# LayerNorm of a residual sum on one core: adds moved to GpSimd, ScalarE and VectorE put into hardware loops

## The chip, the cores and the metric

The kernel runs on one core of one Trainium2 chip. The metric is the time on the device, in microseconds (us), of the slowest (here the only) core. A run is one execution; medians are over several runs of one kernel.

## The reference

```python
# x, residual: 16 x 1024 x 512 float32; gamma, beta: 512
z = x + residual
mean = np.mean(z, axis=-1, keepdims=True)
var = np.var(z, axis=-1, keepdims=True)
return (gamma * (z - mean) / np.sqrt(var + eps) + beta).astype(np.float32)
```

There are 16384 rows of 512 values. Each of the 128 partitions handles 128 of them, so a "row" below means one row in every partition, a tile of 128 x 512. Both inputs are read and the result is written: 100.66 MB pass between the core's SBUF and memory, whatever the kernel does in between. (SBUF is the core's on-chip buffer; PSUM is the one into which TensorE's matmuls write.)

## The kernel before

One buffer holds 64 rows of x, is overwritten by the sum and at last by the result, and is stored from there. Another holds 32 rows of the residual. All large transfers are issued from one queue (SP), loads 40 rows ahead of the stores.

```python
X_CHUNKS = [8] * 15 + [4, 4]      # rows of one load; R_CHUNKS is the same
OUT_CHUNKS = [16] * 7 + [8, 4, 4] # rows of one store
GROUP = 4; Z_ROWS = 64; R_ROWS = 32; STORE_LAG = 40; ADD_PERIOD = 8
```

Seven rows of eight are added by TensorE: two matmuls with an identity matrix sum x and residual in PSUM. ScalarE copies the sum back to SBUF and takes the row's total on the way. The eighth row is added on VectorE.

```python
def add(g):
    ...
        nc.tensor.matmul(ps, ident, zrow(j), start=True, stop=False)
        nc.tensor.matmul(ps, ident, rrow(j), start=False, stop=True)

def copy_then_sqrt(g):
    ...
        nc.scalar.activation(out=zrow(j), in_=PS.pop(j), func=ACT.Identity,
                             accum_out=SM[g][:, j - j0 : j - j0 + 1])
```

VectorE makes the negated mean of four rows. ScalarE squares the centred rows and sums them. VectorE then makes two passes over every row, (z - mean) * gamma and z * rstd + beta, with gamma and beta in SBUF.

```python
def affine1(g):
    ...
        nc.vector.scalar_tensor_tensor(out=zrow(j0 + k), in0=zrow(j0 + k),
            scalar=NM[g][:, k : k + 1], in1=gamma_t, op0=ALU.add, op1=ALU.mult)

def affine2(g):
    ...
        nc.vector.scalar_tensor_tensor(out=zrow(j0 + k), in0=zrow(j0 + k),
            scalar=rstd[:, k : k + 1], in1=beta_t, op0=ALU.mult, op1=ALU.add)
```

Everything is written out: Python loops emit each instruction of all 128 rows.

## Time and profile before

| | before |
|---|---|
| time, median of 3 runs | 242.99 us (242.69 to 243.09) |
| bytes moved by the large transfers | 100.67 MB |
| share of the 16 DMA engines' span in those transfers | 98.1% |
| last load landed (the one before it: 205.9 us) | 210.8 us |
| last VectorE pass ended | 231.2 us |
| end of the profiled execution | 241.0 us |

First come lines of the profile's page of the kernel before. The line "PE 203.2 ..." gives busy time and share of the span by engine, with the number of instructions. DMA cuts the span into 40 slices and gives the busy share of the DMA engines in tenths. The q lines are DMA queues: packets, MB, share of the 16 engines' span. The line with "DVE 53%" is the chain of waits that ended last. Group lines give busy time, mean ns of one, and the engine's idle time before them with what ended it.

```profile
span 241.0 us, 1990 instructions
...
PE 203.2 (84%) x452; PEld 87.6 (36%) x452; DVE 192.7 (80%) x356; ACT 169.8 (70%) x514; POOL 0.7 (0%) x6
...
DMA  7999999999999999999999999999999999999993
...
q1 hardware_dynamic: 6336, 100.67, 98.1%
q8 instruction: 3, 0.05, 0.1%
q14 instruction: 7, 0.06, 0.1%
...
DVE 53%; DMA 19%; PE 17%; issue 3%; ACT 3%; SPq 1%; DVEq 0%
...
L209 DVE SCALAR_TENSOR_TENSOR zbuf<-zbuf,nm,gamma_t 128x512 f32<-128x512 f32 x128 | 89.5, 749 | 12.8 <-ACT junk L185 12.8
...
L224 DVE SCALAR_TENSOR_TENSOR zbuf<-zbuf,rstd,beta_t 128x512 f32<-128x512 f32 x128 | 87.7, 747 | 1.1
...
```

TensorE is busy for 84% of the span, but it does not set the time. The DMA row is at 9 from the second slice to the last but one, and queue q1 alone fills 98.1%. Queues q8 and q14, of the kind "instruction" on the page, move 0.11 MB at 0.1% of the 16 engines' span each. They are called instruction fetches below; e2 and e3 fit that (loops written out took q14 from 2 packets to 6, and a stream of TensorE instructions brought q8 back).

Next is the windows view of the kernel before. A window's columns are its length, busy time of each engine with the number of instructions, TensorE clock, DMA share (1.00 is all 16 engines busy), GB/s.

```profile
...
core 0: us, PE busy (x) PEld busy (x) DVE busy (x) ACT busy (x) POOL busy (x), PEclk, DMA share, GB/s
12.00:226.00 214.00, 197.12 (x446) 86.08 (x446) 185.99 (x344) 168.33 (x513) 0.00 (x0) 0.98 1.01 430
226.00:229.00 3.00, 0.00 (x0) 0.00 (x0) 2.96 (x6) 0.15 (x1) 0.00 (x0) 0.50 0.87 371
236.00:237.00 1.00, 0.00 (x0) 0.00 (x0) 0.00 (x0) 0.00 (x0) 0.00 (x0) 0.50 0.62 262
237.00:238.00 1.00, 0.00 (x0) 0.00 (x0) 0.00 (x0) 0.00 (x0) 0.00 (x0) 0.50 0.37 156
238.00:239.00 1.00, 0.00 (x0) 0.00 (x0) 0.00 (x0) 0.00 (x0) 0.00 (x0) 0.50 0.18 74
...
```

Over 214 us the DMA engines are full (a share of 1.01, 430 GB/s). The last view of this kernel is the SP queue's own waits (total, times, longest).

```profile
...
SPq L81 <- DMA out_dram<-zbuf: 92.6, 4, 27.0
SPq L84 <- DVE zbuf L140: 55.8, 5, 14.9
SPq L87 <- DVE zbuf L224: 44.3, 4, 20.7
...
```

SP waits longest for stores to land, because a load may only overwrite rows that have been stored. It also waits for VectorE (L84 and L87), so this view alone does not settle what binds; with the DMA share of 1.01 it fits a full queue. The chain of waits, which names VectorE first, then names work that hides behind transfers.

### The profile page before, as it was taken

The numbers are of one execution on the slowest core, as the hardware profiler recorded it, in microseconds if no ns is written. First come the engines' busy times: TensorE is split into PE (matmuls) and PEld (weight loads), VectorE is DVE, ScalarE is ACT, GpSimd is POOL, SyncE is SP. The second block draws the span as 40 slices with busy tenths as digits, with TensorE's granted clock in tenths as the row PEclk, the third lists the DMA queues.
The fourth block names the chain that finished last, engine by engine and source line by source line (L and its number), as shares of the span: only waits on it lengthen the run. The fifth ranks groups of instructions, "written<-read, shape, count | busy, mean of one in ns | idle before, by whom it ended". The sixth has DMA issues, their size and how long they took to land.

```text
span 241.0 us, 1990 instructions
## 1 busy us (share of the span) xinstructions
PE 203.2 (84%) x452; PEld 87.6 (36%) x452; DVE 192.7 (80%) x356; ACT 169.8 (70%) x514; POOL 0.7 (0%) x6
## 2 busy tenths in 40 slices
PE   3689999999999999999999996899949999890000
PEld 0134444444444444444444442344414444340000
DVE  1101279999999999999999999739997799989930
ACT  0213699797979797979797979269783888786500
POOL 1000000000000000000000000000000000000000
PEclk9999999999999999999999999799999999997555
DMA  7999999999999999999999999999999999999993
GB/s 262 435 435 435 430 422 419 423 432 431 435 443 432 400 428 432 430 430 430 431 432 443 426 419 427 427 468 405 419 432 430 450 401 419 443 435 435 427 413 160
DMA packets 6350, 100.78 MB, mean 418 GB/s; under 512 B 706, under 2 KB 706, under 8 KB 708
## 3 DMA queue, kind: packets, MB, share of 16 engines
q1 hardware_dynamic: 6336, 100.67, 98.1%
q8 instruction: 3, 0.05, 0.1%
q14 instruction: 7, 0.06, 0.1%
q10 hardware_dynamic: 4, 0.00, 0.0%
HBM read 67.11 MB, written 33.55 MB: 418 GB/s over the span
## 4 chain that ended last, share of the span: by engine, by line
DVE 53%; DMA 19%; PE 17%; issue 3%; ACT 3%; SPq 1%; DVEq 0%
DVE zbuf L209 26%; DVE zbuf L224 23%; DMA rbuf<-in_residual_dram 19%; PE ps L133 9%; PE ps L132 8%; DVE zbuf L140 3%; ACT junk L185 1%; DVE rstd L222 1%; ACT zbuf L156 1%; DVE nm L171 1%; ACT L197 1%; SPq L81 0%; DVEq L312 0%; SPq L87 0%; ACT std L197 0%
## 5 line engine op out<-in xcount | busy, mean ns | idle before, releaser
L133 PE MATMUL ps<-rbuf,ident 128*128 128x512 f32 x224 | 117.5, 607 | 9.4 <-DVE zbuf L209 6.4
L132 PE MATMUL ps<-zbuf,ident 128*128 128x512 f32 x224 | 117.6, 607 | 0.0
L209 DVE SCALAR_TENSOR_TENSOR zbuf<-zbuf,nm,gamma_t 128x512 f32<-128x512 f32 x128 | 89.5, 749 | 12.8 <-ACT junk L185 12.8
L156 ACT ACTIVATE zbuf<-ps 128x512 f32<-128x512 f32 x112 | 66.0, 589 | 46.6 <-PE ps L133 46.5
L185 ACT ACTIVATE junk<-zbuf,nm 128x512 f32<-128x512 f32 x128 | 90.4, 711 | 1.6 <-DVE nm L171 1.6
L224 DVE SCALAR_TENSOR_TENSOR zbuf<-zbuf,rstd,beta_t 128x512 f32<-128x512 f32 x128 | 87.7, 747 | 1.1
L133 PEld LDWEIGHTS ps<-rbuf,ident 128*128 128x128 f32 x224 | 43.0, 194 | 66.4 <-issue 53.0
L132 PEld LDWEIGHTS ps<-zbuf,ident 128*128 128x128 f32 x224 | 43.6, 195 | 56.3 <-issue 43.3
L185 ACT ACTIVATION_READ_ACCUMULATOR junk<-zbuf,nm 128x1 f32 x128 | 24.3, 190 | 0.0
L156 ACT ACTIVATION_READ_ACCUMULATOR zbuf<-ps 128x1 f32 x112 | 21.8, 195 | 0.0
L171 DVE TENSOR_SCALAR nm<-sm 128x4 f32<-128x4 f32 x32 | 5.2, 163 | 13.3 <-ACT zbuf L156 13.3
L140 DVE SCALAR_TENSOR_TENSOR zbuf<-zbuf,rbuf 128x512 f32<-128x512 f32 x16 | 11.0, 685 | 0.0
L197 ACT ACTIVATE std<-ssq,eps_t 128x4 f32<-128x4 f32 x32 | 9.3, 290 | 0.1
L222 DVE RECIPROCAL rstd<-std 128x4 f32<-128x4 f32 x32 | 5.6, 175 | 3.2 <-ACT std L197 3.2
L115 PE MATMUL ps<-gb_row,ones 1*128 1x512 f32 x4 | 4.1, 1129 | 4.8 <-DMA gb_row<-in_gamma_dram 2.7
L156 ACT ACT_TABLE_LOAD x1 | 1.3, 1283 | 8.1 <-DMA zbuf<-in_x_dram 8.1
L116 DVE COPY gamma_t<-ps 128x512 f32<-128x512 f32 x1 | 0.7, 692 | 3.8 <-PE ps L115 3.8
L116 DVE COPY beta_t<-ps 128x512 f32<-128x512 f32 x1 | 0.7, 692 | 3.5 <-PE ps L115 3.5
L115 PEld LDWEIGHTS ps<-gb_row,ones 1*128 1x128 f32 x4 | 1.0, 306 | 6.3 <-DMA gb_row<-in_beta_dram 3.6
L140 DVE DVE_READ_ACCUMULATOR zbuf<-zbuf,rbuf 128x1 f32 x16 | 1.3, 82 | 0.0
L197 ACT ACT_TABLE_LOAD x1 | 1.3, 1283 | 0.0
L104 DVE MEMSET ones<- 1x128 f32 x1 | 0.2, 165 | 0.8 <-PEq L298 0.8
(7 smaller groups left out, 1.0 us busy)
## 6 DMA issues: line engine op xcount, KB each, us to landing
zbuf<-in_x_dram SPq DMA_DIRECT2D x15, 2048.0 KB, 25.3
rbuf<-in_residual_dram SPq DMA_DIRECT2D x15, 2048.0 KB, 20.8
out_dram<-zbuf SPq DMA_DIRECT2D x7, 4096.0 KB, 28.7
zbuf<-in_x_dram SPq DMA_DIRECT2D x2, 1024.0 KB, 33.1
rbuf<-in_residual_dram SPq DMA_DIRECT2D x2, 1024.0 KB, 33.1
out_dram<-zbuf SPq DMA_DIRECT2D x1, 2048.0 KB, 15.5
out_dram<-zbuf SPq DMA_DIRECT2D x2, 1024.0 KB, 10.2
gb_row<-in_gamma_dram ACTq DMA_DIRECT2D x1, 2.0 KB
```

Of the source, the lines that this page charges most:

```text
L115: nc.tensor.matmul(ps, ones, gb_row[:, k, :], start=True, stop=True)
L116: nc.vector.tensor_copy(dest, ps)
L132: nc.tensor.matmul(ps, ident, zrow(j), start=True, stop=False)
L133: nc.tensor.matmul(ps, ident, rrow(j), start=False, stop=True)
L140: nc.vector.scalar_tensor_tensor(out=zrow(j), in0=zrow(j), scalar=0.0, in1=rrow(j), op0=ALU.add, op1=ALU.add, accum_out=SM[g][:, j - j0 : ...
L156: nc.scalar.activation(out=zrow(j), in_=PS.pop(j), func=ACT.Identity, accum_out=SM[g][:, j - j0 : j - j0 + 1],)
L171: nc.vector.tensor_scalar(out=nm[:, :n], in0=SM.pop(g)[:, :n], scalar1=-inv_d, scalar2=None, op0=ALU.mult,)
L185: nc.scalar.activation(out=junk, in_=zrow(j0 + k), func=ACT.Square, bias=NM[g][:, k : k + 1], accum_out=ssq[:, k : k + 1],)
L197: nc.scalar.activation(out=std[:, :n], in_=SSQ.pop(g)[:, :n], func=ACT.Sqrt, bias=eps_t[:, 0:1], scale=inv_d,)
L209: nc.vector.scalar_tensor_tensor(out=zrow(j0 + k), in0=zrow(j0 + k), scalar=NM[g][:, k : k + 1], in1=gamma_t, op0=ALU.add, op1=ALU.mult,)
L222: nc.vector.reciprocal(out=rstd[:, :n], in_=STD.pop(g)[:, :n])
L224: nc.vector.scalar_tensor_tensor(out=zrow(j0 + k), in0=zrow(j0 + k), scalar=rstd[:, k : k + 1], in1=beta_t, op0=ALU.mult, op1=ALU.add,)
```

## The change

The transfers, their order and the buffers are the same. The work on rows is divided anew. GpSimd adds a whole loaded chunk in place. ScalarE reads each row twice from SBUF, first for the negated mean and then for the squares, and writes the unneeded full-size results to PSUM. VectorE has gamma and beta in PSUM, where matmuls with ones put them. TensorE does nothing after that. ScalarE and VectorE run hardware loops of 16 turns of 8 rows, each with its head placed by `head_slot`. Semaphores are counted by hand. (The diff is cut, and some lines are joined.)

```diff
-    for j in range(j0, j0 + n):              # add, rows not on VectorE
-        nc.tensor.matmul(ps, ident, zrow(j), start=True, stop=False)
-        nc.tensor.matmul(ps, ident, rrow(j), start=False, stop=True)
...
+    while lo < total:
+        nc.gpsimd.wait_ge(sx[have_x], 16)
+        nc.gpsimd.wait_ge(sr[have_r], 16)
+        nc.gpsimd.tensor_tensor(
+            out=z, in0=z, in1=part(rbuf, R_ROWS, lo, n), op=ALU.add
+        ).then_inc(s_add, n)
...
+    with act.bass.Fori(
+        0, turns, engines=OrderedEngineSet([act.engine]), head_slot={act.engine: 128}
+    ) as t:
+        ...
+        act.wait_ge(s_add, r0 + TURN)
+        for k in range(2 * TURN):
+            ...
+            if k < TURN:
+                i = act.activation(out=junk[k % JUNK][:, :], in_=row_at(zoff, row),
+                    func=ACT.Identity, scale=-inv_d, accum_out=nm[:, bass.ds(r0 + row, 1)])
+            else:
+                i = act.activation(out=junk[k % JUNK][:, :], in_=row_at(zoff, row),
+                    func=ACT.Square, bias=nm[:, bass.ds(r0 + row, 1)],
+                    accum_out=ssq[:, bass.ds(r0 + row, 1)])
+            i.then_inc(s_act, 1).wait_op(s_act, due, "sem-ge")
+        ...                                   # Sqrt of 8 rows
...
+    with dve.bass.Fori(
+        0, turns, engines=OrderedEngineSet([dve.engine]), head_slot={dve.engine: 128}
+    ) as t:
+        ...                                   # first pass, reciprocal, second pass
-                in1=gamma_t,
+                in1=gamma_p[:, :],
...
-                in1=beta_t,
+                in1=beta_p[:, :],
```

## The prediction

> **What bounds the kernel now.** The transfers. The page's list of DMA queues puts 98.1% of all 16 engines' span on one queue, 100.67 MB in 241.0 us. The windows view shows the DMA share at about 1.00, 426 to 437 GB/s, in nearly every stretch from 12 to 226 us; only the start, 226 to 229 us (0.87) and the last five microseconds (0.62 falling to 0.00) are below. 100.67 MB at 430 GB/s is 234 us. The chain of waits names VectorE (53%), but its 192.7 us of work hide behind the full DMA queue: the store queue's longest waits are for stores to land (92.6 us). The last loads land at 205.9 us, VectorE's last row is done at 231.2, and the DMA stays full until 236.
>
> **What the change removes, adds and moves.** 448 matmuls, 112 ScalarE copies out of PSUM and 16 VectorE adds go. GpSimd adds whole chunks of 8 rows. ScalarE makes the negated mean in a scaled Identity pass, then Square, both from SBUF to PSUM. VectorE keeps two passes per row, gamma and beta now in PSUM. The 44 large transfers and their order are unchanged.
>
> Cost of 8 rows (estimates):
> - GpSimd: [...] No such add is in the trace. [...]
> - ScalarE: Square starts every 0.705 us in the timeline, Identity from PSUM every 0.57, from SBUF perhaps 0.62. 8 x 1.32 + 0.2 for the root = 10.8 us.
> - VectorE: four passes take 2.65 us on the chain, 0.66 each. [...] plus 0.6 for reciprocal, waits and loop turn: about 12 us.
> - DMA: 6.29 MB at 430 GB/s: 14.6 us.
>
> So every engine stays under the DMA's pace. [...]
>
> **On the critical path.** Nearly nothing in the middle: the first output comes later, but some 15 us of queued loads stand before the first store. At the tail, from the last landing at about 206 us: [...] Identity 5, Square 6, plus the backlog of the turn before; I expect VectorE to end at about 233 us, so the last store starts some 2 us later, partly hidden by queued stores. Saved: 0.3% of DMA time of instruction fetch, and the 0.4 us dip at 226.
>
> **Predicted: 242.8 us, 240.5 to 248 in 8 of 10; faster by over 2% 0.03, within 2% 0.84, slower 0.13.**
>
> **What will show it.** Right: DMA about 98% and 1.00 in the middle windows; [...] ScalarE near 170 us, VectorE 170 to 195, PE near 0; VectorE ending at 231 to 235. Wrong: DMA share below 0.95 before 220 us; 1 us idle or more at each loop turn.
>
> **What would make it wrong.** VectorE above about 13 us per turn [...]: then VectorE ends after 240 us and the time follows. Faster than 240 only if the final drain shortens.

Cut from the recorded text, where marked, is what no trace of this case showed when it was written: the cost of GpSimd's add, per chunk and at the tail, a surcharge for VectorE's PSUM sources, the reason for gamma and beta in PSUM, a sentence on loop turns, and suspected causes of failure. The sums still contain these terms, so what stands does not add up to them. The turn of VectorE came to about 12 us: 16 passes at the 0.66 us of the trace make 10.6, 0.6 is the estimate for the reciprocal, waits and the loop's turn, with no source given, and the surcharge came on top. The upper end of 195 us busy contains it too. VectorE's end came to about 233 us, with the add, and with a backlog for which no figure was given. That GpSimd stays under the transfers' pace was shown only by the changed kernel (8.86 us per chunk).

## The result, and the profile after

Four runs of the changed kernel had a median of 242.07 us (241.97 to 242.40), and four of the kernel before, in the same rounds, 243.04 us (242.69 to 243.32). The ratio is 0.9968, with a 95% interval from 0.9953 to 0.9984. Ratios here are those that the timing program gave, worked out from the fast runs of the same rounds; they are not quite the ratios of the medians (here 0.9960) or of the plain means (0.9963) of these runs. The change is faster by 0.3%: the same within 2%, but clear of noise.

The page of the changed kernel, the same lines as before:

```profile
span 240.3 us, 1855 instructions
...
PE 4.1 (2%) x4; PEld 1.0 (0%) x4; DVE 178.7 (74%) x274; ACT 176.6 (73%) x529; POOL 142.1 (59%) x21
...
DMA  7999999999999999999999999999999999999994
...
q1 hardware_dynamic: 6336, 100.67, 98.3%
q14 instruction: 2, 0.02, 0.0%
...
DMA 56%; ACT 14%; issue 13%; POOL 6%; DVE 3%; SPq 2%; ACTq 2%; DVEq 0%; POOLq 0%
...
L158 POOL TENSOR_TENSOR zbuf<-zbuf,rbuf 128x4096 f32<-128x4096 f32 (+1 forms) x17 | 141.9, 8348 | 72.2 <-DMA rbuf<-in_residual_dram 72.2
L221 DVE SCALAR_TENSOR_TENSOR zbuf<-zbuf,nm,gamma_p 128x512 f32 x128 | 91.0, 748 | 51.5 <-ACT junk L193 50.0
...
L234 DVE SCALAR_TENSOR_TENSOR zbuf<-zbuf,rstd,beta_p 128x512 f32 x128 | 85.7, 743 | 0.6
...
```

The two VectorE groups take 0.75 us per pass, as before. GpSimd's line mixes 15 adds of 4096 columns with two of 2048; by form they took 8858 and 4524 ns. No compute engine is busy for more than 74% of the span. The DMA row and the 98.3% of q1 are as before. Instruction fetch is down to one line with 0.02 MB. The chain of waits now names transfers.

The windows view of the changed kernel (columns as before):

```profile
...
12.00:226.00 214.00, 0.00 (x0) 0.00 (x0) 172.76 (x263) 175.31 (x528) 141.92 (x17) 1.00 1.01 430
226.00:229.00 3.00, 0.00 (x0) 0.00 (x0) 2.96 (x6) 0.00 (x0) 0.00 (x0) 1.00 0.89 382
236.00:237.00 1.00, 0.00 (x0) 0.00 (x0) 0.00 (x0) 0.00 (x0) 0.00 (x0) 1.00 0.80 336
237.00:238.00 1.00, 0.00 (x0) 0.00 (x0) 0.00 (x0) 0.00 (x0) 0.00 (x0) 1.00 0.14 57
238.00:239.00 1.00, 0.00 (x0) 0.00 (x0) 0.00 (x0) 0.00 (x0) 0.00 (x0) 1.00 0.04 16
...
```

The middle is unchanged. The dip at 226 to 229 us is still there. The difference is after 236 us: the engines stop nearer to each other. Before, shares of 0.37 and 0.18 were left in the two microseconds after 237; now they are 0.14 and 0.04.

The SP queue's own waits of the changed kernel:

```profile
...
SPq L131 <- DMA out_dram<-zbuf: 111.2, 4, 29.7
SPq L145 <- DVE zbuf L234: 65.2, 7, 29.0
SPq L137 <- POOL zbuf L158: 35.9, 4, 17.0
...
```

SP waits a little longer in total for stores to land (111.2 us against 92.6 us). Waits for compute have grown too, but the queue behind them was never empty in the windows above.

**Where the 0.8 us came from.** Each large transfer raises its semaphore in 16 steps, and the trace has the time of every step. I take the steps to be one for each of the 16 DMA engines: the same distances come back in transfer after transfer (the two largest are 2.6 and 3.0 us in each of the last four loads of e2). I call the distance of the last of the 16 from their median the lag. It tells how far the most delayed DMA engines are behind the rest. The final store of 1 MB ends the program, so its last step counts and not its median. I worked the following table out of the traces (all in us from the first instruction; "fetches" are instruction-fetch packets of 8 KB or more that began between 12 and 237 us).

```
kernel             median step   last step   lag    span     fetches
before                237.06       239.88    2.82   240.96   10, of these 3 of 16 KB
changed               237.32       239.05    1.73   240.33    1
```

The bulk of the final store landed 0.26 us later in the changed kernel (its first load was issued at 0.94 us, before at 0.74). Its last step landed 0.83 us earlier, because the lag is 1.09 us shorter. That is the whole gain, and a little more. (Lags are read from one profiled run of each kernel. The changed kernel gave 1.73 us here and 1.51 us in e9, so differences of a few tenths mean nothing.) Six of the 16 steps were more than 1.3 us behind the median before, and two are now.

I took two theories to the chip. **Theory A**: instruction fetches take time on the same DMA engines (in the kernel before, packets of 8 KB took 0.31 to 0.33 us between 12 and 237 us, those of 16 KB 1.00 to 1.10 us); in a kernel that keeps the engines full, a delayed one never catches up, and the program ends with the most delayed one. **Theory B**: the gain comes from the new division of the work, with TensorE silent and another order of work at the end.

### The profile page after: what moved, and what is told of

Read it like the earlier page. It is cut to its first block, busy times and chain, and to the rows that moved or that the text cites. A ratio compares the mean times of both kernels' runs of the same rounds, so it can differ in the third digit from the quotient of the medians.

```text
span 240.3 us, 1855 instructions
## 1 busy us (share of the span) xinstructions
PE 4.1 (2%) x4; PEld 1.0 (0%) x4; DVE 178.7 (74%) x274; ACT 176.6 (73%) x529; POOL 142.1 (59%) x21
## 3 DMA queue, kind: packets, MB, share of 16 engines
q1 hardware_dynamic: 6336, 100.67, 98.3%
## 4 chain that ended last, share of the span: by engine, by line
DMA 56%; ACT 14%; issue 13%; POOL 6%; DVE 3%; SPq 2%; ACTq 2%; DVEq 0%; POOLq 0%
DMA out_dram<-zbuf 36%; DMA rbuf<-in_residual_dram 20%; ACT junk L193 9%; POOL zbuf L158 6%; ACT junk L185 5%; DVE zbuf L234 3%; SPq L131 1%; ACTq L183 1%; ACTq L185 1%; SPq L137 1%; ACT std L202 0%; SPq L145 0%; DVE rstd L230 0%; DVEq L234 0%; ACTq L171 0%
## 5 line engine op out<-in xcount | busy, mean ns | idle before, releaser
L158 POOL TENSOR_TENSOR zbuf<-zbuf,rbuf 128x4096 f32<-128x4096 f32 (+1 forms) x17 | 141.9, 8348 | 72.2 <-DMA rbuf<-in_residual_dram 72.2
L221 DVE SCALAR_TENSOR_TENSOR zbuf<-zbuf,nm,gamma_p 128x512 f32 x128 | 91.0, 748 | 51.5 <-ACT junk L193 50.0
L185 ACT ACTIVATE junk<-zbuf 128x512 f32 x128 | 74.5, 582 | 46.0 <-POOL zbuf L158 43.0
L193 ACT ACTIVATE junk<-zbuf,nm 128x512 f32 x128 | 86.2, 674 | 0.0
L234 DVE SCALAR_TENSOR_TENSOR zbuf<-zbuf,rstd,beta_p 128x512 f32 x128 | 85.7, 743 | 0.6
L193 ACT ACTIVATION_READ_ACCUMULATOR junk<-zbuf,nm x128 | 24.2, 189 | 0.0
L185 ACT ACTIVATION_READ_ACCUMULATOR junk<-zbuf x128 | 23.9, 187 | 0.0
L202 ACT ACTIVATE std<-ssq,eps_t x16 | 4.8, 301 | 1.6
L230 DVE RECIPROCAL rstd<-std x16 | 3.1, 196 | 0.0
L110 PE MATMUL beta_p<-gb_row,ones 1*128 1x512 f32 x2 | 2.1, 1136 | 2.4 <-DMA gb_row<-in_beta_dram 2.4
```

The lines of the kernel that those rows point to most:

```text
L110: nc.tensor.matmul(dest[:, :], ones[:, :], gb_row[:, k * D : (k + 1) * D], start=True, stop=True).then_inc(s_pe, 1)
L158: nc.gpsimd.tensor_tensor(out=z, in0=z, in1=part(rbuf, R_ROWS, lo, n), op=ALU.add).then_inc(s_add, n)
L185: i = act.activation(out=junk[k % JUNK][:, :], in_=row_at(zoff, row), func=ACT.Identity, scale=-inv_d, accum_out=nm[:, bass.ds(r0 + row, 1)],)
L193: i = act.activation(out=junk[k % JUNK][:, :], in_=row_at(zoff, row), func=ACT.Square, bias=nm[:, bass.ds(r0 + row, 1)], accum_out=ssq[:, ...
L202: act.activation(out=std[:, bass.ds(r0, TURN)], in_=ssq[:, bass.ds(r0, TURN)], func=ACT.Sqrt, bias=eps_t[:, 0:1], scale=inv_d,).then_inc(s ...
L221: dve.scalar_tensor_tensor(out=row_at(zoff, k), in0=row_at(zoff, k), scalar=nm[:, bass.ds(r0 + k, 1)], in1=gamma_p[:, :], op0=ALU.add, op1 ...
```

## The experiments

Eleven kernels were run, all with repeated timing against the kernel before on the same chip. Each edit is against the changed kernel.

### e1: the transfers alone

```diff
-            wait_rows(s_add, "add", rlo + rn - R_ROWS)   # and: wait_rows(s_out, "out", olo + on)
+            # wait for the landing of the loads that used these rows
-    (all GpSimd, ScalarE and VectorE work on rows)
```

> The changed kernel without its compute (wrong result on purpose): the same 44 large transfers in the same order, each waiting only for the landings it depends on. If both kernels are bound by the transfers (theory A and B alike): 241.2 to 242.2 us, at most 1 us under the changed kernel's 242.07, DMA share 98% or more. If compute holds back the changed kernel somewhere: 238 us or less. Theory A (instruction fetches delay single DMA engines, and the last store ends with the most delayed engine) expects a lag of the last of the 16 landings of the final store behind their median of 1.8 us or less (1.73 in the changed kernel, 2.82 in the one before).

Measured: 241.25 us (241.21 to 241.34), ratio 0.9933; lag 0.42 us. Its output is wrong, which doesn't matter for the time. Lines of its page:

```profile
span 239.2 us, 126 instructions
...
q1 hardware_dynamic: 6336, 100.67, 98.7%
...
q14 instruction: 1, 0.00, 0.0%
...
```

The floor of these transfers in this order is 241.25 us. The changed kernel stands 0.8 us above it and the kernel before 1.7 us. With this order of transfers and these waits between them, that is all that a change to the compute alone could gain. The bulk of the final store landed at 237.32 us, exactly as in the changed kernel; all of the difference between the two last steps is lag.

### e2: both loops written out

```diff
-    with act.bass.Fori(0, turns, ..., head_slot={act.engine: 128}) as t:
+    for t in range(turns):
-    with dve.bass.Fori(0, turns, ..., head_slot={dve.engine: 128}) as t:
+    for t in range(turns):
```

> The changed kernel with both hardware loops written out; same division of the work, same semaphores. Theory A (the 0.8 us come from fewer instruction fetches, which ride on the DMA engines): about six more fetches of 8 KB, each 0.3 to 0.6 us of delay to the engine that carries it; lag of the final store 2.0 to 2.6 us, time 242.3 to 242.9. Theory B (the 0.8 us come from the other division of the work: TensorE idle, no SBUF or PSUM traffic of matmuls, another tail): no loop is needed, time 241.9 to 242.2, lag as in the changed kernel.

Measured: 243.12 us (243.06 to 243.36), ratio 1.001; lag 2.96 us, six fetches. Correct. Lines of its page:

```profile
span 241.4 us, 1004 instructions
...
q1 hardware_dynamic: 6336, 100.67, 97.9%
q14 instruction: 6, 0.05, 0.0%
...
```

This is the division of the work of the changed kernel, and all of its gain is gone. Theory B falls. The size was larger than I expected of theory A (243.12 against at most 242.9): 0.05 MB of fetches cost 1 us. The steps can be watched. This table, worked out of the trace, gives for each fetch the two largest distances from the median in the transfer that landed before it or as it began, and in a transfer that landed soon after it (us):

```
fetch of 8 KB at   before        after
 37.5              0.16  0.19    0.16  0.58
 59.6              0.15  0.57    0.55  0.94
 81.6              0.55  1.11    1.15  1.36
118.6              1.58  1.62    1.58  2.31
147.7              1.57  2.31    2.31  2.56
176.4              2.29  2.56    2.56  2.98
```

Each of the six fetches is followed by a step, and in the loads no distance is made up for later. Two things do not fit a simple sum. The steps, 0.4 to 1.0 us for each fetch over the two engines, are longer than the 0.31 us that a fetch packet itself took in the trace. And there are rises with no recorded fetch beside them: one from 0.94 to 1.11 at about 72 us, and one from 1.16 and 1.36 to 1.56 and 1.63 at about 100 us. Whether the trace holds every fetch is not known.

### e3: an idle instruction stream on TensorE

```diff
+    for c in range(len(loads_x)):
+        nc.tensor.wait_ge(sx[c], 16)
+        for k in range(13):
+            m = nc.tensor.matmul(pe_junk[:, :1], ones[:, :], gb_row[:, :1], start=True, stop=True)
```

> The changed kernel plus 221 one-column matmuls on the otherwise idle TensorE, 13 after each landed chunk of x, written to a spare PSUM bank: about the number of TensorE instructions of the kernel before (some 880), nothing waits for them. Theory A: three or four more fetches of 16 KB, which cost the engine that carries one up to 1.6 us: lag 2.2 to 3.3 us, time 242.4 to 243.2. Theory B: 241.9 to 242.2, because these matmuls move almost no data.

Measured: 242.64 us (242.39 to 242.91), ratio 0.9991; lag 2.17 us. Correct. The 1.6 us of the expectation fits the kernel before: from the load that landed at 47.0 us to that at 51.9 us (medians) the lag there went from 0.14 to 1.65 us, with a fetch of 8 KB at 45.3 us and one of 16 KB at 47.3 us. Three packets of 16 KB on q8 came back, a queue that the changed kernel does not use. Adding instructions that do nothing useful, move almost no data and delay no transfer took away more than half of the gain by the ratios; the intervals still touch (0.9979 to 1.0003 here, 0.9953 to 0.9984 for the changed kernel). This run also keeps TensorE busy for 101 us, so by itself it does not tell fetches from an active TensorE; e2 and e11, with TensorE idle, do. The first 16 KB fetch, at 42.5 us, was followed by a step from under 0.1 to 1.53 us on one engine. The latest engine rose to 2.1 us between 67 and 72 us with no recorded fetch beside it, and the two later fetches left its distance as it was.

### e4: both

The edits of e2 and e3 together.

> Loops written out and the idle TensorE stream, both: the number of fetched instructions of the kernel before with the division of the work of the changed one. Theory A: the whole gain is gone, 242.7 to 243.4 us, lag 2.5 to 3.3 us. Theory B: 241.9 to 242.2.

Measured: 242.98 us (242.96 to 243.29), ratio 1.0008 to the kernel before, whose runs of the same rounds had a median of 242.98 too; lag 2.44 us, nine fetches. Correct. The instruction traffic of the kernel before, on the changed division of work, gives the time before. With nine fetches it is not slower than e2 with six. That fits that the most delayed engine counts and not the sum of the fetches; the trace does not name the engine that carried a fetch.

### e5: a small add

```diff
-        z = part(zbuf, Z_ROWS, lo, n)
+        z = part(zbuf, Z_ROWS, lo, n)[:, :16]
-            out=z, in0=z, in1=part(rbuf, R_ROWS, lo, n), op=ALU.add
+            out=z, in0=z, in1=part(rbuf, R_ROWS, lo, n)[:, :16], op=ALU.add
```

> The changed kernel, but each GpSimd add covers 16 columns of its chunk and not 4096 (wrong result on purpose): the chain stays, the GpSimd work of 8.9 us per chunk goes. If the lag that is left in the changed kernel (1.73 us, against 0.42 without any compute) comes from GpSimd's traffic in SBUF: lag 0.4 to 0.9 us, time 241.2 to 241.7. If it comes from the instruction fetches at the loops' start and from something that GpSimd has no part in: lag 1.4 to 1.9 us, time 241.8 to 242.3. That the compute ends some 4.5 us earlier is worth nothing in either, if the transfers bind.

Measured: 242.18 us (242.05 to 242.46), ratio 0.9953; lag 2.13 us. Its output is wrong, which doesn't matter for the time. The lag in the profiled run, the slowest of the five (242.46 us), was larger than either branch expected: a miss. GpSimd's traffic is not its source, since the lag is there without it. Taking 8.9 us of latency out of each chunk's chain bought nothing beyond the noise.

### e6: gamma and beta in SBUF

```diff
+    dve.tensor_copy(gamma_t[:, :], gamma_p[:, :]).then_inc(s_copy, 1)
+    dve.tensor_copy(beta_t[:, :], beta_p[:, :]).then_inc(s_copy, 1)
+    dve.wait_ge(s_copy, 2)
-                in1=gamma_p[:, :],        # and beta_p
+                in1=gamma_t[:, :],        # and beta_t
```

> The changed kernel with gamma and beta copied from PSUM to SBUF, so VectorE's passes read two tensors from SBUF beside GpSimd. [...] VectorE and GpSimd block each other, a VectorE pass waits up to 8.9 us for a chunk's add, a turn of VectorE goes from 11.3 to 16 us or more, and the time to 255 us or more. [...] the GpSimd add 10 to 14 us, VectorE passes up to 1 us, time within 242 to 250. If there is no contention: 242.0 to 242.3, and PSUM was not needed for that.

The first branch has each engine wait for the other's whole work, the second has them take turns.

Measured: 331.47 us (331.34 to 331.65), ratio 1.3625. Correct. Groups of instructions by form, as on the page:

```profile
...
L240 DVE SCALAR_TENSOR_TENSOR zbuf<-zbuf,rstd,beta_t 128x512 f32 x128 | 179.1, 1471 | 0.6
L158 POOL TENSOR_TENSOR zbuf<-zbuf,rbuf 128x4096 f32<-128x4096 f32 x15 | 149.5, 9976 | 96.5 <-DMA rbuf<-in_residual_dram 96.5
L227 DVE SCALAR_TENSOR_TENSOR zbuf<-zbuf,nm,gamma_t 128x512 f32 x128 | 115.7, 974 | 18.3 <-ACT junk L193 18.3
...
```

And its timeline (start, us, instruction, count):

```profile
...
118.26 5.38 DVE L227 SCALAR_TENSOR_TENSOR zbuf<-zbuf,nm,gamma_t 128x512 f32 x8
...
118.78 13.53 POOL L158 TENSOR_TENSOR zbuf<-zbuf,rbuf 128x4096 f32<-128x4096 f32 x1 [36.81 <-DMA rbuf<-in_residual_dram]
...
123.80 9.06 DVE L240 SCALAR_TENSOR_TENSOR zbuf<-zbuf,rstd,beta_t 128x512 f32 x1
```

One VectorE pass, which takes 0.75 us undisturbed, took 9.06 us, as long as a GpSimd add. One add, begun while VectorE was in a row of passes, took 13.53 us and not 8.86. The add waited for the whole row of passes, which ended at 123.6 us, and the next pass then waited for the whole add: it ended at 132.9 us, 0.55 us after it. So they do not take turns pass by pass. Over the run, 16 passes took more than 1 us (4.6 to 9.3), and the four adds that began in a row of passes took 11.1 to 13.5 us. The page of this run shows what that did to the transfers:

```profile
...
DMA  7999999960029999999008999999404990822966
...
q1 hardware_dynamic: 6336, 100.67, 73.0%
...
```

The DMA share fell from 98% to 73%. So gamma and beta in PSUM are what lets GpSimd add without loss beside these passes: with them there, adds took 8.86 us and passes 0.743 and 0.748 us on average. Expected was 255 us or more; how much more was not worked out, so the 331 us was not predicted.

### e7: a slower ScalarE

```diff
+EXTRA = 4
-        for k in range(2 * TURN):
+        for k in range(EXTRA + 2 * TURN):      # the first EXTRA passes write to a spare column
```

> The changed kernel with 4 more sum passes (0.61 us each) per turn on ScalarE, results thrown away: a turn of 13.8 us, still below the transfers' 14.6 us. If only the mean pace counted: time as in the changed kernel, 242 to 243. As predicted (above about 13 us per turn the time follows, because ScalarE starts at 22 us and has 16 turns to do): ScalarE ends near 243 us, VectorE near 249 us, time 253 to 258.

Measured: 255.79 us (255.71 to 256.32), ratio 1.0519. Correct. VectorE ended at 248.9 us, where 249 had been expected. ScalarE's turn of 13.8 us was shorter than the 14.6 us that the transfers take for 8 rows (6.29 MB at the measured 430 GB/s), and the kernel still became bound by compute. ScalarE begins only after the first chunk has landed and been added, at 22.9 us, and 16 turns of 13.8 us from there end after the transfers.

### e8: loop heads not placed

```diff
-        0, turns, engines=OrderedEngineSet([act.engine]), head_slot={act.engine: 128}
+        0, turns, engines=OrderedEngineSet([act.engine])        # the same for VectorE
```

> The changed kernel without the placing of the loop heads. Theory A: [...]more fetches than the 8 of the changed kernel, by up to 30, lag 2.5 us or more and time 242.8 or more, with ScalarE or VectorE idle of 1 us or more at the turns. [...]no more fetches, 241.7 to 242.3. Theory B (division of the work): 241.9 to 242.3 in either case, as long as the turns stay below 13 us.

The first branch of theory A has more fetches without the placing, the second (241.7 to 242.3 us) has no more.

Measured: 242.40 us (242.22 to 242.50), ratio 0.9962; lag 1.61 us, one fetch. Correct. The time lies 0.1 us above the branch without more fetches, but the kernel before was slower in these rounds as well (243.24 us), and the ratio equals that of the changed kernel. Here the placing was worth nothing; no run shows a case in which it pays.

### e9, e10, e11: what is left

e9 is the changed kernel once more. e10 runs the loops of the changed kernel beside the transfers of e1 on buffers of their own:

```diff
+    za, zv, zw: buffers of 1, 8 and 8 rows; R_ROWS = 16 to make room
-                    in_=row_at(zoff, row),
+                    in_=za[:, :],
-                out=row_at(zoff, k), in0=row_at(zoff, k),
+                out=zv[:, k * D : (k + 1) * D], in0=za[:, :],      # second pass: zw
```

e11 has only ScalarE's loop written out, with the first half of the edit of e2.

> The changed kernel itself once more, on the chip of the next two runs, so that they have it as a neighbour. 241.9 to 242.4 us, ratio to the kernel before 0.995 to 0.998, lag 1.4 to 2.2 us (1.73 in its first profile).

Measured: 242.14 us (241.83 to 242.50), ratio 0.9971; lag 1.51 us, one fetch.

> The transfers alone, as in the run without compute, while the two hardware loops run beside them on buffers of their own (wrong result on purpose; the residual buffer is 16 rows, to make room). Nothing that the transfers wait for depends on the loops, but their instructions are fetched and run. If the lag that is left in the changed kernel comes with the execution of the loops: lag 1.2 to 2.0 us, time 241.7 to 242.3. If it needs that compute and transfers touch the same buffers or wait for each other: lag below 0.9 us, time 241.2 to 241.6.

Measured: 242.59 us (242.18 to 243.01), ratio 0.9991; lag 1.45 us in the profiled run, which took 242.18 us; one fetch. Its output is wrong, which doesn't matter for the time. The time missed both branches. The lag was as the first branch said, but the profiled run was the fastest of the five; the others had spans of 240.7 to 241.2 us, so, with a span without lag of 238.8 us, lags of about 1.9 to 2.4 us (an estimate). The smaller residual buffer did not hold the transfers up: the median step of the final store came at 237.29 us, in e1 at 237.32. So a lag beyond the floor, as large as that of the changed kernel, does not need any coupling of compute and transfers. It comes with running the loops. What carries it is open: after 23 us it grew from 0.79 to 1.45 us, and no fetch is recorded there. The changed kernel shows the same: from 0.86 us at 18 us to 1.73 us, with no recorded fetch after 13.7 us. This kernel, with one fetch, lost about as much of the gain as e3 did with four, so fetches are not the only thing that makes lag.

> Only ScalarE's loop written out, VectorE's loop kept. Theory A: about four recorded fetches of 8 KB more than in the changed kernel, lag 2.0 to 3.0 us, time 242.4 to 243.2, between the changed kernel and the one with both loops written out (243.12). Theory B: as the changed kernel, within 0.2 us of its neighbour run.

Measured: 243.19 us (242.98 to 243.45), ratio 1.0009; lag 2.67 us, five fetches. Correct. ScalarE's loop alone makes the difference, on a second chip and beside e9 (242.14 us, ratio 0.9971). Writing out VectorE's loop as well (e2) added nothing to that.

### All together

Spans and steps of the profiled runs, worked out of the traces (us):

```
kernel              median time   span     lag    span - lag   fetches, 12 to 237 us
before                 243.04    240.96   2.82    238.14       10
changed                242.07    240.33   1.73    238.60        1
e1 transfers alone     241.25    239.23   0.42    238.81        0
e2 both written out    243.12    241.42   2.96    238.46        6
e3 TensorE stream      242.64    240.72   2.17    238.55        4
e4 both                242.98    241.05   2.44    238.61        9
e5 small add           242.18    240.69   2.13    238.56        1
e8 heads not placed    242.40    240.28   1.61    238.67        1
e9 changed again       242.14    240.05   1.51    238.54        1
e10 detached loops     242.59    240.26   1.45    238.81        1
e11 ScalarE out        243.19    241.18   2.67    238.51        5
```

The lag and the span are those of one profiled run, which need not be the median one. The span without the lag stays within 0.7 us, though e1 has no compute at all. The lag runs from 0.42 to 2.96 us. In e6 and e7, where the DMA queue ran empty near the end, the lag of the final store was 0.10 and 0.08 us, which fits that an engine that gets a pause catches up.

## Why the prediction was right or wrong

**The transfers bind: right.** The transfers alone need 241.25 us. DMA share in the middle was 1.01, and q1's share 98.3%, as predicted.

**Costs of a turn: right, nearly all.** GpSimd took 8.86 us per chunk and was busy for 142 us. ScalarE took 11.33 us per turn (10.8): the two kinds of pass came every 0.61 and 0.705 us, as estimated, and the root with the loop's turn took 0.8 us and not 0.2. VectorE was predicted to be the slower of the two at about 12 us; it keeps to ScalarE's 11.33 us. These two lines, of the timeline of the kernel before and of the changed one, show passes with the second tensor in SBUF and in PSUM:

```profile
...
92.98 2.74 DVE L224 SCALAR_TENSOR_TENSOR zbuf<-zbuf,rstd,beta_t 128x512 f32<-128x512 f32 x4
...
```

```profile
...
102.21 5.36 DVE L234 SCALAR_TENSOR_TENSOR zbuf<-zbuf,rstd,beta_p 128x512 f32 x8
107.70 5.68 DVE L221 SCALAR_TENSOR_TENSOR zbuf<-zbuf,nm,gamma_p 128x512 f32 x8
...
```

Four passes of 0.747 us in 2.74 us start every 0.66 us; eight of 0.743 us in 5.36 us also start every 0.66 us. The first pass, at 5.68 us for eight, is held by ScalarE's squares, one every 0.705 us. So a PSUM source cost no more than one in SBUF here; the surcharge for it was not there.

**No contention with gamma and beta in PSUM: right**. Adds took 8.86 us and passes 0.75 us in the changed kernel; in e6, with two tensors from SBUF, they took up to 13.53 and 9.3 us.

**The limit of about 13 us per turn: fits, but was tested on one side only.** No run lies between 11.33 and 13.8 us per turn. e7 at 13.8 us lost 13.7 us to the changed kernel (255.79 less 242.07; the two were timed on different chips).

**The tail: VectorE's end was near by luck.** It ended at 231.8 us, predicted 233. But the sum behind that began at the wrong load: at 205.9 us the last residual but one had landed in the kernel before, the last one at 210.8 us, and in the changed kernel at 209.9 us. The "backlog of the turn before" was not there either: ScalarE was idle for 2.81 us until the last add was done. The two errors nearly cancelled. Of the steps after the landing, the add took 4.52 us; the other two were sized well (Identity 4.9 us, for 5; Square 5.7, for 6). Lines of the changed kernel's timeline:

```profile
...
210.07 4.52 POOL L158 TENSOR_TENSOR zbuf<-zbuf,rbuf 128x2048 f32<-128x2048 f32 x1 [0.50 <-DMA rbuf<-in_residual_dram]
...
214.86 0.60 ACT L185 ACTIVATE junk<-zbuf 128x512 f32 x1 [2.81 <-POOL zbuf L158]
...
226.43 5.36 DVE L234 SCALAR_TENSOR_TENSOR zbuf<-zbuf,rstd,beta_p 128x512 f32 x8
```

The last store was issued 0.6 us later than before, where 2 us had been expected, and queued stores hid it: the bulk of the final store landed 0.26 us later, and 0.2 us of that matches the later first load.

**Why 242.8 was predicted and 242.07 measured: the terms of the sum.** The prediction saved "0.3% of DMA time of instruction fetch" (0.7 us of 241 us) and the 0.4 us dip, and came out only 0.2 us below the kernel before. So some 0.9 us must have stood for the tail (an estimate of mine; the prediction gives no figure). Measured were 1.09 us less lag, no dip saved (0.87 before, 0.89 after) and at most 0.26 us for the tail. **The tail is the term that was mis-sized most**; the missed saving at the dip hid part of that. The fetch term came near in size for a wrong reason. The prediction took it as an average over 16 engines, and for that 0.3% was too much: the page has 0.1% on each of q8 and q14. The average is the wrong measure. The program ends with its latest DMA engine, and delays add up on a few: 2.82 us of lag became 1.73.

**The idle time of 1 us or more at each loop turn, named as a sign of being wrong, did not come**; ScalarE's idle time before a turn was about 0.27 us.

Open are the carrier of the lag that grows without a recorded fetch (part of the 1.0 us between e1 and e10), why a step is longer than the fetch packet beside it, and whether the recording of instructions for the profile adds to the lag. The number of recorded instructions alone does not order the lags: e2 has 1004 of them and 2.96 us, the changed kernel 1855 and 1.73 us.

## What to carry to other kernels

In a kernel bound by transfers (here a DMA share of 1.01 over 214 us), ask which DMA engine ends last and not how busy they are on average: compare the last of a final transfer's completion steps with their median. In e2 each fetch of 8 KB was followed by a delay of 0.4 to 1.0 us over the two latest engines, and the loads did not make it up; the final store's lag was 2.96 us. Shorter programs (hardware loops, an idle engine left without code) had only that lag to win: here 1.1 of 2.8 us. Before moving work to GpSimd, see how many tensors VectorE beside it reads from SBUF: here the kernel took 242.07 us with one and 331.47 us with two (e6; ratios to the kernel before 0.9968 and 1.3625). And check the slack of a stage from its start time plus turns and not from its mean pace (e7: a turn of 13.8 us against the transfers' 14.6, and 255.79 us).
